# A T5-bias table for dilated attention: rows stored once and repeated from DRAM to DRAM

## The chip, the core and the metric

The kernel runs on one core of a Trainium2 chip, in one launch. The metric is the time of the whole program on the device in microseconds (us), lower is better. Five engines work side by side, each in its own order and tied to the others by semaphores: TensorE (PE, with its weight loads as PEld), VectorE (DVE), ScalarE (ACT), GpSimd (POOL) and SyncE (SP, which only issues transfers). Transfers are issued by SP, ACT or POOL into their own queues and carried out by DMA engines.

## The reference

One decoder layer over 2048 tokens of width 1024. What matters here is the input projection and the bias of the dilated attention:

```python
proj = h @ w_in[i]
r_in, k_in, v_in, q_at, k_at, v_at = jnp.split(proj, splits, axis=-1)
y_rwkv = rwkv7_mix(h, r_in, k_in, v_in, ...)
y_att = dilated_attention(to_heads(q_at), to_heads(k_at), to_heads(v_at), rel_bias)

def dilated_branch(q, k, v, rel_bias, window, dil):    # for (128, 1), (512, 4), (2048, 16)
    ...
    rel = np.arange(blk)[:, None] + blk - np.arange(2 * blk)[None, :]
    bias = jnp.transpose(rel_bias[t5_bucket(np.clip(rel, 0, None) * dil)], (2, 0, 1))
    logits = jnp.einsum('bdhnqc,bdhnkc->bdhnqk', qs, kb) * (HEAD_DIM ** -0.5) + bias[None, None, :, None]
    logits = jnp.where(valid, logits, NEG_INF)
```

For each of three patterns and each of 8 heads the bias depends on the distance of query and key alone, so one row of 384 numbers holds all of it; a block of 128 queries by 256 keys reads that row with a shift of one for each query. After the attention come an output projection, layer norms, a router with 32 experts, and a gated embedding.

## The kernel before, in words

The program goes through stages: `project` (the input projection, and the preparation of the RWKV inputs), `mixers` (RWKV and attention woven together), `mix_out`, `route`, `ple`, `experts`, `finish`. Products of float32 are made of three matmuls of split operands (lines 196 to 200).

The change is in the part of `project` that makes the RWKV keys and the attention values (lines 455 to 488), some 350 to 590 us from the start. It runs in steps. A step makes one 128x512 piece of the key (24 matmuls; ScalarE writes a scaled copy `sh` at L285, VectorE adds into `o` at L287, SP stores `o` at L290), squares it on ScalarE (`sq`, L458), makes two pieces of the values (24 matmuls each; ScalarE copies them to `ov`, L452; SP stores them, L453), and between these the norm of the key: PE sums `sq` into `pn` (L462), VectorE and ScalarE make the reciprocal root, and SP stores `rn` (L468). Four steps make one column block of the key weights. In each four, SP loads the weights of the next block (`wr`, L255).

The tiles `sh`, `ov` and others share one tag of the pool `st` with two buffers, so a tile waits until the one two places back is free, and an `ov` is free when its store has landed.

The bias table is made beside these steps by a generator, `attn_bias`. At the end of each step the loop calls it once (`next(bias, None)`, L486), and it runs to its next `yield`. For a pattern it loads constants on POOL's queue, multiplies them on PE (L965), subtracts on VectorE (L966) into `br` (8 partitions, a head each, of 384 numbers), and stores `br` 128 times over on ACT's queue (L967) into the DRAM tensor `biasrow` (8 heads, 3 patterns, 128 rows, 384). Much later `load_bias` (L995) reads from it with a row step of 383, which gives the shift, 128x2x256 for two heads.

PE's order in `project` is that of the code (`manual_schedule`); the other engines' order, and all in `mixers`, is set by a scheduler that simulates the program. Transfers from SP and ACT take eight completion semaphores in turn (named DMAHW0 to DMAHW7 below); before a transfer takes one again, its queue waits until the last transfer that used it has landed.

Of the kernel before, what the change touches and what calls it, by code (L numbers as in the profile page):

```python
# [18 lines left out]
P = 128  # L19
# [148 lines left out]
class K:  # L168
# [784 lines left out]
    def attn_bias(self, tile, bank):  # L953

        nc, I = self.nc, self.I
        L = 3 * P
        self.biasrow = rows = self.scratch("biasrow", (8, 3, P, L))
        for n in range(3):
            hot, br = tile(32, L + 8, "hot"), tile(8, L, "br")
            nc.gpsimd.dma_start(hot[:, 0:L], I["hot"][:, n])  # L960
            nc.gpsimd.dma_start(hot[:, L:], I["rel_bias"])
            nc.gpsimd.dma_start(br, I["gone"][:, n])
            yield
            ps = bank()
            nc.tensor.matmul(ps[0:8, 0:L], hot[:, L:], hot[:, 0:L], start=True, stop=True)  # L965
            nc.vector.tensor_tensor(out=br, in0=br, in1=ps[0:8, 0:L], op=ALU.subtract)  # L966
            nc.scalar.dma_start(rows[:, n], br.unsqueeze(1).to_broadcast([8, P, L]))  # L967
            yield
            yield
            yield  # L970

    def attn_open(self, es):
        self.al, self.ap = (es.enter_context(self.tc.tile_pool(name=name, bufs=1, reuse_waits="tile")) for name in ("al", "ap"))
# [1022 lines left out]
```

## Time and profile before

| | |
|---|---|
| time, median of 3 runs | 3246.5 us (3241.99 to 3250.48) |
| the profiled execution | 3253.92 us, its span 3252.1 us |
| PE busy | 2928.5 us, 90% of the span |
| VectorE, ScalarE busy | 2113.1 us, 1526.9 us |
| DMA, mean | 164 GB/s |
| mean granted TensorE clock | 0.928 of full speed |
| the three bias stores | 1536 KB each, issued at 373.1, 437.5 and 502.0 us |

Times inside the program count from the start of the span. A wait is the idle time of an engine ahead of an instruction, put down to what ended it. In a row of the timeline the bracket gives that wait. The queue of SP's transfers is q1, that of ACT's is q10.

### The profile page before, as it was taken

How to read it: one execution, taken by the hardware profiler on the slowest of the kernel's cores; microseconds unless marked ns; L12 is line 12 of the kernel's file. 1: busy time of each engine (PE TensorE's matmuls, PEld its weight loads, DVE VectorE, ACT ScalarE, POOL GpSimd, SP SyncE). 2: the span in 40 equal slices, each digit the busy share in tenths (PEclk: the TensorE clock that was granted, in tenths of full speed). 3: DMA queues.
4: the chain of work that ended last, by engine and by line, in shares of the span. 5: the costliest groups of instructions: out<-in, count | busy, mean ns of one | idle time of the engine just before them, and what ended most of it. 6: DMA issues, size and time to landing. Idle time of an engine off the chain costs nothing. (4 is left out here: it accounts for less than half of the span.)

```text
span 3252.1 us, 49914 instructions
## 1 busy us (share of the span) xinstructions
PE 2928.5 (90%) x17038; PEld 2335.2 (72%) x17039; DVE 2113.1 (65%) x4730; ACT 1526.9 (47%) x3650; POOL 675.3 (21%) x682
## 2 busy tenths in 40 slices
PE   8989888999798998998997899899999999998880
PEld 6666777777687777777786677788777777776560
DVE  4997333686564755666657678653587787766756
ACT  3444211555454544544444233311477777765642
POOL 0442000244100312112102122223011111112216
PEclk9999989999799889988898899999999999999885
DMA  5212433688725335235205453243499999987845
GB/s 166 80 56 95 103 88 80 203 273 266 154 60 123 100 79 132 69 76 139 65 22 144 138 177 123 96 140 94 175 307 323 324 304 322 313 295 225 289 130 210
DMA packets 364064, 533.09 MB, mean 164 GB/s; under 512 B 92376, under 2 KB 204640, under 8 KB 363792
## 3 DMA queue, kind: packets, MB, share of 16 engines
q1 hardware_dynamic: 330144, 459.09, 44.4%
q0 software_dynamic: 14496, 45.93, 6.0%
q10 hardware_dynamic: 19168, 24.86, 3.1%
q8 instruction: 136, 2.23, 0.3%
q14 instruction: 120, 0.98, 0.1%
HBM read 402.27 MB, written 128.06 MB: 163 GB/s over the span
## 5 line engine op out<-in xcount | busy, mean ns | idle before, releaser
L1711 DVE TENSOR_TENSOR wl<-raw,wh 128x512 fp32r<-128x512 f32 x768 | 478.0, 681 | 88.5 <-ACT wh L1710 87.9
L1710 ACT CAST wh<-raw 128x512 fp32r<-128x512 f32 x768 | 417.5, 620 | 12.2 <-DMA raw<-in_w_up_dram 10.5
L198 PE MATMUL ps<-xh,wh 128*128 128x512 f32 x640 | 263.1, 411 | 0.3 <-ACT xh L322 0.3
L199 PE MATMUL ps<-xl,wh 128*128 128x512 f32 x640 | 259.2, 405 | 0.9 <-DVE xl L323 0.8
L200 PE MATMUL ps<-xh,wl 128*128 128x512 f32 x640 | 257.9, 403 | 0.0
L1088 ACT ACTIVATE pe<-pe,ms 128x256 f32<-128x256 f32 (+1 forms) x384 | 174.9, 457 | 161.0 <-DVE ms L1085 153.3
L1840 POOL DMA_INDIRECT acc<-ysb,ix x48 | 96.5, 2010 | 623.0 <-ACT ysb L1839 402.6
L198 PE MATMUL pe<-wh,XX 128*128 128x512 f32 x480 | 199.3, 415 | 3.8 <-ACT wh L1710 3.8
L199 PE MATMUL pe<-wl,XX 128*128 128x512 f32 x480 | 191.8, 400 | 2.6 <-DVE wl L1711 2.6
L200 PE MATMUL pe<-wh,XX 128*128 128x512 f32 x480 | 190.7, 397 | 0.0
L198 PEld LDWEIGHTS ps<-xh,wh 128*128 128x128 f32 x640 | 125.1, 195 | 34.2 <-issue 2.8
L199 PEld LDWEIGHTS ps<-xl,wh 128*128 128x128 f32 x640 | 124.7, 195 | 29.9 <-DVE xl L323 2.3
L200 PEld LDWEIGHTS ps<-xh,wl 128*128 128x128 f32 x640 | 124.5, 194 | 29.6
L1094 PE MATMUL pl<-eye,pe 128*128 128x128 f32 x600 | 128.6, 307 | 10.1 <-ACT pe L1088 9.5
L1069 PE MATMUL pl<-KK,Q 128*128 128x256 f32 x432 | 116.4, 395 | 20.3 <-DMA KK<-ks 8.2
L1108 PE MATMUL po<-pe,V 128*64 128x128 f32 x1200 | 123.0, 309 | 8.6 <-DVE O L1122 7.0
L198 PE MATMUL pb<-gh,XH 128*128 128x512 f32 x320 | 126.0, 394 | 0.0
L199 PE MATMUL pb<-gl,XH 128*128 128x512 f32 x320 | 125.2, 391 | 0.0
L1755 PE MATMUL pe<-wh,XX 128*128 128x512 f32 x288 | 120.1, 417 | 5.4 <-ACT wh L1710 5.4
L200 PE MATMUL pb<-gh,XL 128*128 128x512 f32 x320 | 124.8, 390 | 0.0
L1756 PE MATMUL pe<-wl,XX 128*128 128x512 f32 x288 | 118.4, 411 | 3.0 <-DVE wl L1711 3.0
L198 PE MATMUL pa<-woh,YH 128*128 128x512 f32 x256 | 112.5, 439 | 3.1 <-ACT YH L1338 3.1
(418 smaller groups left out, 7565.2 us busy)
## 6 DMA issues: line engine op xcount, KB each, us to landing
raw<-in_w_gate_dram SPq DMA_DIRECT2D x128, 512.0 KB
raw<-in_w_up_dram SPq DMA_DIRECT2D x128, 512.0 KB
raw<-in_w_down_dram SPq DMA_DIRECT2D x128, 512.0 KB
pk<-pk SPq DMA_DIRECT2D x32, 512.0 KB
pk_t<-pk SPq DMA_DIRECT2D x32, 512.0 KB
KK<-ks SPq DMA_DIRECT2D x64, 256.0 KB
wr<-in_w_in_dram SPq DMA_DIRECT2D x48, 256.0 KB
rkk<-rkk SPq DMA_DIRECT2D x32, 384.0 KB
```

The costliest lines, as they stand in the source:

```text
L198: mm(out, lh, rh, start=first, stop=False)
L199: mm(out, lh, rl, start=False, stop=False)
L200: mm(out, ll, rh, start=False, stop=last)
L1069: mm(pl[:, h], q, toks(KK[:, m, h], n, prev, 2), start=m == 0, stop=m == 1)
L1088: nc.scalar.activation(pe[:, h, w], pe[:, h, w], AF.Exp, bias=m_[h], scale=-1.0, accum_out=s_[h])
L1094: nc.tensor.transpose(pt[:, h, b], pe[:, h, b * P:(b + 1) * P], self.c("eye"))
L1108: mm(o[h * 64:(h + 1) * 64, j], vb[:, h * 64:(h + 1) * 64], tt[:, h, b], start=b == kb[0], stop=b == 1)
L1710: nc.scalar.copy(wh[:, c], raw[:, c])
L1711: nc.vector.tensor_tensor(out=wl[:, c], in0=raw[:, c], in1=wh.bitcast(F32)[:, c], op=ALU.subtract)
L1755: mm(ps, L[:, 0:P], wh, start=first, stop=False)
L1756: mm(ps, L[:, 0:P], wl, start=False, stop=last)
L1840: nc.gpsimd.indirect_dma_start(out=self.acc, out_offset=bass.IndirectOffsetOnAxis(ap=ix[0:r, e, b:b + 1], axis=0), in_=ysb[0:r], in_offset ...
```

## The change

`attn_bias` stores `br` once, 8 rows of 384 numbers, into a new DRAM tensor `biasone`. In its next two turns it issues four copies from there to `biasrow`, DRAM to DRAM, two heads each and 128 times over, two in each turn. The number of turns for a pattern stays at four. All five transfers are on ACT's queue.

```diff
         self.biasrow = rows = self.scratch("biasrow", (8, 3, P, L))
+        one = self.scratch("biasone", (8, 3, L))
         for n in range(3):
...
             nc.vector.tensor_tensor(out=br, in0=br, in1=ps[0:8, 0:L], op=ALU.subtract)
-            nc.scalar.dma_start(rows[:, n], br.unsqueeze(1).to_broadcast([8, P, L]))
+            nc.scalar.dma_start(one[:, n], br)
             yield
-            yield
-            yield
+
+            for h in range(0, 8, 2):
+                nc.scalar.dma_start(rows[h:h + 2, n], one[h:h + 2, n].unsqueeze(1).to_broadcast([2, P, L]))
+                if h % 4:
+                    yield
```

ScalarE at the first pattern, before (semaphores that an instruction waits for stand in brackets; PE_49, DVE_49 and Activation_49 are the engines' own):

```order
L452 COPY ov<-ps 128x256 [waits PE_49,Activation_49]
L967 DMA biasrow<-br 8x128x384 [waits DMAHW2_49,DVE_49]
L285 ACTIVATE sh<-ps,prm 128x512 [waits DMAHW0_49,PE_49,Activation_49]
L458 ACTIVATE sq<-o,prm 128x512 [waits DVE_49]
L452 COPY ov<-ps 128x256 [waits DMAHW1_49,PE_49,Activation_49]
```

And the same place with the change (lines behind 967 are moved by up to 4):

```order
L452 COPY ov<-ps 128x256 [waits PE_49,Activation_49]
L968 DMA biasone<-br 8x384 [waits DMAHW2_49,DVE_49]
L972 DMA biasrow<-biasone 2x128x384 [waits DMAHW2_49]
L972 DMA biasrow<-biasone 2x128x384
L972 DMA biasrow<-biasone 2x128x384 [waits DMAHW6_49]
L285 ACTIVATE sh<-ps,prm 128x512 [waits DMAHW0_49,PE_49,Activation_49]
L972 DMA biasrow<-biasone 2x128x384 [waits DMAHW7_49]
L458 ACTIVATE sq<-o,prm 128x512 [waits DVE_49]
L452 COPY ov<-ps 128x256 [waits DMAHW1_49,PE_49,Activation_49]
```

The scheduler put three of the four copies right behind the small store and the fourth behind `sh`; the first copy waits for the small store (DMAHW2).

SP's queue behind that place, before, from the store of `rn` in the step of the bias store on:

```order
L468 DMA rkk<-rn 128x512 [waits DMAHW3_49,DVE_49]
L290 DMA rkk<-o 128x512 [waits DMAHW4_49,DVE_49]
L453 DMA va<-ov 128x256 [waits DMAHW5_49,Activation_49]
L453 DMA va<-ov 128x256 [waits DMAHW6_49,Activation_49]
L468 DMA rkk<-rn 128x512 [waits DMAHW7_49,DVE_49]
L255 DMA wr<-in_w_in_dram 128x4x128 [waits DMAHW0_49,DVE_49]
L255 DMA wr<-in_w_in_dram 128x4x128 [waits DMAHW1_49,DVE_49]
L290 DMA rkk<-o 128x512 [waits DMAHW2_49,DVE_49]
L453 DMA va<-ov 128x256 [waits DMAHW3_49,Activation_49]
```

And with the change:

```order
L468 DMA rkk<-rn 128x512 [waits DMAHW3_49,DVE_49]
L290 DMA rkk<-o 128x512 [waits DMAHW0_49,DVE_49]
L453 DMA va<-ov 128x256 [waits DMAHW1_49,Activation_49]
L453 DMA va<-ov 128x256 [waits DMAHW2_49,Activation_49]
L468 DMA rkk<-rn 128x512 [waits DMAHW3_49,DVE_49]
L255 DMA wr<-in_w_in_dram 128x4x128 [waits DMAHW4_49,DVE_49]
L255 DMA wr<-in_w_in_dram 128x4x128 [waits DMAHW5_49,DVE_49]
L290 DMA rkk<-o 128x512 [waits DMAHW6_49,DVE_49]
L453 DMA va<-ov 128x256 [waits DMAHW7_49,Activation_49]
```

The order on SP is the same. Its semaphores are others: the bias store had DMAHW2, and the copies now have DMAHW4 to DMAHW7, which the last four rows wait for.

In `mixers` rows change their neighbours. PE near its begin, before (`pl` are attention's products, the others RWKV's):

```order
L1069 MATMUL pl_7362<-KK,Q 128x256
L822 MATMUL ps_7369<-pk_t 128x128 x4
L834 MATMUL ps_7555<-eye,v_t 128x128 x2
L725 MATMUL ps_7559<-eye,pk_t 128x128 x2
L822 MATMUL ps_7370<-pk_t 128x128 x4
L1072 MATMUL pl_7344<-KK,Q 128x256 x2
L1069 MATMUL pl_7355<-KK,Q 128x256 x3
```

And with the change:

```order
L1073 MATMUL pl_7375<-KK,Q 128x256
L822 MATMUL ps_7382<-pk_t 128x128 x4
L834 MATMUL ps_7568<-eye,v_t 128x128 x2
L725 MATMUL ps_7572<-eye,pk_t 128x128 x2
L1076 MATMUL pl_7357<-KK,Q 128x256 x2
L1073 MATMUL pl_7368<-KK,Q 128x256 x3
L1073 MATMUL pl_7375<-KK,Q 128x256 x3
L822 MATMUL ps_7383<-pk_t 128x128 x4
```

Products of attention stand here ahead of four matmuls of RWKV that were ahead of them; there are more such exchanges down to the end of the stage, and no instruction is added or taken away there.

## Rows read from the trace of the kernel before

**Rows 1.** The page, busy time of each engine.

```profile
PE 2928.5 (90%) x17038; PEld 2335.2 (72%) x17039; DVE 2113.1 (65%) x4730; ACT 1526.9 (47%) x3650; POOL 675.3 (21%) x682
```

**Rows 2.** Stretches around the first bias store: length, busy time, clock, DMA share.

```profile
core 0: us, PE busy (x) PEld busy (x) DVE busy (x) ACT busy (x) POOL busy (x), PEclk, DMA share, GB/s
376.00:390.00 14.00, 14.00 (x88) 12.26 (x87) 4.86 (x4) 3.66 (x7) 0.00 (x0) 1.00 0.52 77
390.00:404.00 14.00, 2.18 (x19) 1.97 (x17) 2.68 (x5) 1.27 (x3) 0.00 (x0) 0.71 0.50 76
404.00:410.00 6.00, 5.53 (x22) 4.50 (x23) 2.72 (x2) 1.42 (x3) 0.52 (x1) 0.55 0.68 183
```

**Rows 3.** Waits from 370 to 425: total us, times, longest.

```profile
POOL br L962 <- DMA biasrow<-br: 35.8, 1, 35.8
DVE sh L284 <- DMA va<-ov: 15.3, 1, 15.3
PE pn L462 <- ACT sq L458: 12.3, 1, 12.3
ACT sh L285 <- DMA va<-ov: 10.7, 1, 10.7
```

**Rows 4.** Timeline of ScalarE from 362 to 447: start, us, what.

```profile
365.71 0.72 ACT L458 ACTIVATE sq<-o,prm 128x512 f32<-128x512 f32 x1 [0.82 <-DVE o L287]
...
373.10 0.55 ACTq L967 DMA_DIRECT2D biasrow<-br  x1
377.29 0.69 ACT L285 ACTIVATE sh<-ps,prm 128x512 f32<-128x512 f32 x1 [6.15 <-PE ps L200]
378.79 0.72 ACT L458 ACTIVATE sq<-o,prm 128x512 f32<-128x512 f32 x1 [0.82 <-DVE o L287]
...
400.97 0.69 ACT L285 ACTIVATE sh<-ps,prm 128x512 f32<-128x512 f32 x1 [10.70 <-DMA va<-ov]
...
443.15 0.73 ACT L458 ACTIVATE sq<-o,prm 128x512 f32<-128x512 f32 x1 [0.82 <-DVE o L287]
```

**Rows 5.** SP's issues: timeline, then all stores of L453.

```profile
367.45 4.04 SPq L453 DMA_DIRECT2D va<-ov  x2
373.76 0.32 SPq L468 DMA_DIRECT2D rkk<-rn  x1
378.79 0.32 SPq L290 DMA_DIRECT2D rkk<-o  x1
...
384.26 3.69 SPq L453 DMA_DIRECT2D va<-ov  x1
...
L453 SPq DMA_DIRECT2D va<-ov x32: 319/320/3837, 355.3 to 589.6; - x32
```

**Rows 6.** Timeline of ScalarE from 546 to 572, undisturbed steps.

```profile
547.08 0.73 ACT L458 ACTIVATE sq<-o,prm 128x512 f32<-128x512 f32 x1 [0.82 <-DVE o L287]
559.21 0.72 ACT L458 ACTIVATE sq<-o,prm 128x512 f32<-128x512 f32 x1 [0.82 <-DVE o L287]
571.33 0.73 ACT L458 ACTIVATE sq<-o,prm 128x512 f32<-128x512 f32 x1 [0.82 <-DVE o L287]
```

**Rows 7.** Waits from 360 to 560: PE, then SP's queue.

```profile
PE pn L462 <- ACT sq L458: 36.7, 3, 12.3
...
SPq L290 <- DMA biasrow<-br: 3.6, 3, 1.2
```

**Rows 8.** DMA queues from 373 to 411: packets, MB, share of 16 engines.

```profile
q10 hardware_dynamic: 1032, 1.57, 35.9%
```

**Rows 9.** The same of SP's queue, one store of 1 KB rows (371.6:372.6), one of 2 KB (361.9:363.1).

```profile
q1 hardware_dynamic: 144, 0.13, 37.4%
...
q1 hardware_dynamic: 144, 0.26, 57.5%
```

**Rows 10.** The same of ACT's queue from 22 to 23.4, mostly `slotlist`.

```profile
q10 hardware_dynamic: 68, 0.70, 119.1%
```

**Rows 11.** POOL: its issue ahead of `br`, and DMA issues from 360 to 560.

```profile
372.23 0.50 POOL L961 DMA_DIRECT2D hot<-in_rel_bias_dram  x1
...
hot<-in_rel_bias_dram POOLq DMA_DIRECT2D x2, 1.0 KB, 1.8
br<-in_gone_dram POOLq DMA_DIRECT2D x2, 12.0 KB, 3.0
```

**Rows 12.** Issues with `biasrow`: ns min/median/max, first and last start.

```profile
L1002 SPq DMA_DIRECT2D bias<-biasrow x12: 360/371/537, 814.7 to 1553.7; - x12
L967 ACTq DMA_DIRECT2D biasrow<-br x3: 271/290/548, 373.1 to 501.9; - x3
```

**Rows 13.** The stretch of attention and RWKV, columns as in rows 2.

```profile
815.00:1720.00 905.00, 843.67 (x7196) 682.17 (x7193) 548.45 (x2053) 433.45 (x1500) 136.51 (x250) 0.90 0.38 91
```

**Rows 14.** ACT's issues of `mul`: ns min/median/max, first and last start.

```profile
L242 ACTq DMA_DIRECT2D mul<-in_mu_lora_dram x3: 447/1252/2491, 8.6 to 11.3; - x3
```

## The prediction

> **What bounds the kernel now.** I read the page's totals first: TensorE (PE) is busy 90% of the span, so an edit to the bias rows is worth something only where PE stands still because of them [rows 1]. Then the stretches around the first of the three bias stores, issued at 373.10 (called T from here). The reader is to see PE full until 390, 2.18 of 14 us busy from 390 to 404, and a granted clock of 0.55 just behind it, that is, mostly its lower level of 1.2 GHz instead of 2.4 [rows 2]. The waits of that stretch say what ended the stall: PE's `pn` waited 12.3 us for ScalarE's `sq`, VectorE and ScalarE waited 15.3 and 10.7 us for a store `va<-ov`, and POOL's next load of `br` waited 35.8 us for the bias store itself [rows 3]. So `sh` of L285, which needs the buffer of an `ov` two tiles back, starts at 400.97 = T+27.9 [rows 4]. The stores are ordinary ones of 128 KB. The one issued at 384.26 kept SP 3.69 us at its issue, against a median of 320 ns [rows 5].
>
> What such a stall costs comes from equal steps. Undisturbed, `sq` follows `sq` after 12.12 us (547.08 to 559.21 to 571.33) [rows 6]; with the small bias matmul in it a step takes 13.08 (365.71 to 378.79). Four steps with one such matmul are 3 x 12.12 + 13.08 = 49.4 us; from 378.79 to 443.15, with a bias store in them, they are 64.4 [rows 4, 6]. That is 15.0 us for each pattern, 45 us for three (PE's wait on `sq` is 36.7 us in three from 360 to 560, the longest 12.3 [rows 7]).
>
> **The change part by part.** What is removed: three stores of 1024 rows of 1536 B, read out of 8 partitions. The transfer queue of ACT (q10) shows 1032 packets from 373 to 411: 1024 rows and 8 short endings, while an SP store of 128 rows shows 144, that is 128 and 16 [rows 8, 9]. So a transfer whose first dimension is 8 ran on 8 of the 16 DMA engines, 128 rows on each, and the share of busy DMA engines of about a half agrees [rows 2]. One row took 35.9% x 16 x 38 us / 1032 = 212 ns.
>
> What is added: three stores of 12 KB, and twelve copies of 2 x 128 rows. The twelve are DRAM to DRAM, and their first dimension is 2.
>
> How many engines a copy gets is the main question. The row says 8 engines for 8 and 16 for 128, so I take two engines for 2, and 128 rows on each: all four copies of a pattern put 512 rows on the same two engines, where before 128 rows lay on each of eight.
> The Trainium skill, "DMA: Bandwidth & Descriptors", section "Rules for kernel authors", says that an outermost dimension of size c below 16 confines the whole transfer to at most c engines, and the section "Why a DMA increments its semaphore by 16 and not by 1" adds that they are the lowest-numbered ones. By that rule two engines carry all of it; the 1032 packets agree for c = 8, and no run here shows c = 2.
>
> What one row costs from DRAM to DRAM the trace doesn't show at this size. Nearest rows: SP's stores take 37.4% x 16 x 1 us / 128 = 47 ns for 1 KB and 57.5% x 16 x 1.2 us / 128 = 86 ns for 2 KB [rows 9], so 1.5 KB lies near 65 ns. The only DRAM to DRAM copy of the kernel, `slotlist`, fills most of a stretch with 119.1% x 16 x 1.4 us for 0.70 MB (packets count where they begin), 38 us/MB, or 59 ns for a row [rows 10]. The upper end is the 212 ns of now. I take 65, since both nearest rows lie there and the 212 belongs to eight engines reading eight neighbouring partitions; 59 and 212 stay as ends.
>
> The sum for one pattern, from T: the small store issues in 0.3 us and lands in about 2.5 (POOL's transfers of 1 KB and 12 KB land in 1.8 and 3.0 [rows 11]); three issues take some 0.6 us until the first rows run; then 512 x 65 ns = 33.3 us. The last row is through at T+36.7. ScalarE waits for the landing of the small store, T+0.3 to T+2.8; its next work is `sh` at T+4.2 [rows 4], so that wait is covered, with 1.4 us left.
>
> Now the SP stores behind these rows. Each is spread over all 16 engines, so it ends only when its share on the two engines is through. Before, the store was released at T+27.9, 7.5 us ahead of the end of POOL's wait for the bias store (372.7 + 35.8 = T+35.4) [rows 3, 4, 11], that is with some 35 of 128 rows left. With 35 rows of 65 ns left, 2.3 us ahead of T+36.7, the release is T+34.4; an undisturbed `sh` would be at T+16.3 (377.29 + 12.1). So the stall stays and ends 6.5 us later than now; I take 6, since part of the copies may be issued later and let a store in between. Three patterns: +18 us. The tail with the low clock stays as it is. Twelve issues against three, at 0.27 to 0.55 us each as now [rows 12], lie in the same stall.
>
> Where a copy goes on the queue matters too. SP's transfers take eight completion semaphores in turn, and a transfer waits for the last one that used its own; SP already waits for `biasrow<-br` in this way, 3.6 us in three times [rows 7]. Now two loads `wr`, a store `rkk<-o` and the next step's first `va<-ov` stand in turn behind the four copies. Behind that `va<-ov` on SP everything is queued, and the `sh` of the second step waits for it. If the first stall has already cost 18 us, that store is due at T+38 and loses nothing much.
>
> Moved: the bias loads of attention come 400 us later (814.7 at the earliest [rows 12]) and don't notice. In attention and RWKV (815 to 1720 us) the scheduler gives many rows another neighbour; the instructions are the same, and PE is busy 843.67 of 905 us there [rows 13]. I take 0 and bound it by a sixth of the 61 us that are idle: 10 us either way.
>
> Sum: the profiled execution took 3253.9 us (span 3252.1), so it would be 3272. That execution is 7.4 us above the median of the runs, 3246.5; on the median the forecast is 3246.5 + 18 = **3265 us**.
>
> **The rivals.**
> (a) The stores of SP slip in between the rows, and only the semaphores hold. A store may be 9.8 us late before `sh` feels it (`ov` stored at 367.45, its buffer taken by `sh` at 377.29 [rows 4, 5]). For: in the stretch of the bias store SP's rows did get through in part, since two of its stores were issued in the normal 0.32 us [rows 5]. Against: the 15.3 us wait. Then the last copy lands at T+36.7 plus 2.5 for SP's own share and 2 to land, T+41; the `va<-ov` behind it lands at T+44; the `sh` that needs it would be at T+28.4; 15.6 us late, against 11.6 now (400.97 against 389.4): +4 for a pattern, +12, 3258 us. At 59 ns a row, 3.1 us less: +3, 3249.
> The Trainium skill, "DMA: Bandwidth & Descriptors", section "Queues, rings and completion order", says that a DMA engine goes round its queues packet by packet, 9 to 17 rows typical, 64 at most. By that a store would wait 1.1 to 4.2 us at 65 ns, and this rival would hold; today's 15.3 us wait stands above the 64 x 212 ns = 13.6 us that the same rule gives, so the trace speaks for it only at its ceiling.
> (b) Faster: the copies are spread over all 16 engines and the stall goes. For: what makes a row cost 212 ns now may be the eight source partitions, and they are gone. A pattern's 1024 rows would be 64 rows on each engine, 4.2 us, under the slack of 9.8. It gives back 45 us: 3202. Against: the eight endings. It decides from four times as many endings; on two engines a row would have to cost under 51 ns for any gain ((27.9 - 3.4) / 477), below every row measured.
> (c) A row from DRAM to DRAM costs what it costs now, 212 ns: 108 us for a pattern, which is longer than the 64 us between patterns. By the sum of (a) the `va<-ov` lands near T+119, 91 us late and 79 more than now for a pattern: +237, 3484 us. For it: each row is read and written in DRAM. Against: `slotlist`.
> (d) ScalarE is held at the issue. Of three element-wise loads in a row the third issue took 2491 ns [rows 14]; a third and fourth copy may wait 4 to 8 us each until an earlier one's rows are handed out, and `sh` and `sq` stand behind them. PE then stops earlier, but the end of the pattern is still set by the 512 rows, so it is inside the forecast's range.
>
> **How the numbers follow.** Forecast with (d) 0.52 (+10 to +30), (a) 0.22 (+2 to +12), (b) 0.14, (c) and other prices over 85 ns 0.12. Leaving out (b) and the dear end of (c) leaves about 0.78 inside. Low end: (a) at 59 ns, +3, less the 10 of the moved rows, 3239. High end: 85 ns a row (the price of 2 KB), 10 us more for a pattern than at 65: 3246.5 + 18 + 30 = 3295. I call 0.3%, some 10 us, what a measurement can tell. Faster is (b) and a sliver of (a), 0.16; within 0.3% is most of (a) and the low edge of the forecast, 0.20; slower the rest, 0.64.
>
> **What would show it.** In the profile after: q10 with 128 + 128 rows and 2 endings for each copy, 1032 packets and some 16 more for a pattern, with a DMA share near 0.2 instead of 0.5 for over 30 us behind each small store. PE's wait on `sq` stays at 12 us or more, or splits in two, three times; the wait named is `va<-ov` or `biasrow<-biasone`, on SP too. 16 endings a copy, or a PE without a gap at 385 to 410, would make the forecast wrong; a share of 0.2 for 100 us would be (c).

## The result, and the profile after

The changed kernel takes 3267.9 us (median of 10 runs) against 3246.4 of the kernel before: ratio 1.0054, 95% interval 1.0035 to 1.0072, so some 11 to 23 us slower. One of the ten runs of the kernel before took 8884 us; it hardly moves the median and has no part in the ratio. Run again (experiment 8) the ratio was 1.0070 [1.0044, 1.0096]. The forecast was 3265 and slower. The time was right, and so was the length of the transfers; the step by which they were to cost it was not.

The stretches around the first pattern, to be read beside [rows 2] (the small store is now issued at T = 371.94, 1.2 us earlier than the bias store before; columns as there):

```profile
376.00:390.00 14.00, 2.90 (x25) 2.69 (x23) 0.81 (x2) 0.69 (x1) 0.00 (x0) 0.69 0.18 66
390.00:404.00 14.00, 10.52 (x46) 8.65 (x47) 4.81 (x4) 1.99 (x4) 0.00 (x0) 0.70 0.23 84
404.00:410.00 6.00, 5.63 (x37) 4.73 (x36) 2.31 (x4) 2.71 (x5) 0.00 (x0) 1.00 0.49 158
```

TensorE used to stop from 390 to 404; now it stops from 376 to 390, in the very step of the small store. The DMA share is 0.18 to 0.23 instead of 0.5: few engines are at work, for longer. The granted clock is 0.69 and 0.70 in the first two stretches, so partly at its lower level of 1.2 GHz, and back at 2.4 GHz in the third.

Who waits, from 370 to 425, against [rows 3] (total us, times, longest):

```profile
PE pn L462 <- ACT sq L458: 15.0, 2, 14.6
ACT sh L285 <- issue: 14.4, 1, 14.4
...
ACT sq L458 <- issue: 7.7, 1, 7.7
```

No wait for `va<-ov` is left. ScalarE's `sh` and `sq` are late, and "issue" says that ScalarE waited for nothing that the profile shows. Its own timeline shows what it did (start, us, what; against [rows 4]):

```profile
364.55 0.72 ACT L458 ACTIVATE sq<-o,prm 128x512 f32<-128x512 f32 x1 [0.82 <-DVE o L287]
...
371.94 0.54 ACTq L968 DMA_DIRECT2D biasone<-br  x1
373.35 10.86 ACTq L972 DMA_DIRECT2D biasrow<-biasone  x3
384.33 0.69 ACT L285 ACTIVATE sh<-ps,prm 128x512 f32<-128x512 f32 x1 [14.35 <-issue]
384.36 8.30 ACTq L972 DMA_DIRECT2D biasrow<-biasone  x1
392.70 0.72 ACT L458 ACTIVATE sq<-o,prm 128x512 f32<-128x512 f32 x1 [7.68 <-issue]
...
406.12 0.68 ACT L285 ACTIVATE sh<-ps,prm 128x512 f32<-128x512 f32 x1
...
431.75 0.72 ACT L458 ACTIVATE sq<-o,prm 128x512 f32<-128x512 f32 x1 [0.82 <-DVE o L287]
```

Three issues take 10.86 us and the fourth 8.30, where an issue took 0.27 to 0.55 [rows 12]. ScalarE stands in them, and `sh`, `sq`, the matmuls of `pn` behind `sq`, and all later products stand behind ScalarE. From `sq` at 364.55 to `sq` at 431.75 four steps take 67.2 us, against 64.4 before and 49.4 undisturbed.

SP's stores by line, against the last row of [rows 5], where one issue took 3837 ns:

```profile
L453 SPq DMA_DIRECT2D va<-ov x32: 319/320/339, 354.2 to 596.2; - x32
```

SP's waits on the copies' semaphores from 360 to 560, against the second of [rows 7]:

```profile
SPq L453 <- DMA biasrow<-biasone: 3.5, 3, 1.7
```

And ScalarE's transfer queue from 373 to 411, against [rows 8] (packets, MB, share of 16 engines):

```profile
q10 hardware_dynamic: 1032, 1.57, 11.2%
```

No store of L453 is held at its issue now, and SP waits 1.7 us at most for a copy. The 1032 packets are 1024 rows and two endings for each of the four copies (the small store's 16 lie ahead of 373). So each copy runs on 2 engines, and a row takes 11.2% x 16 x 38 / 1032 = 66 ns.

How far the loss lies in this stage is read from two rows: the sixteen `sq` of L458, and the first load of a bias block (first and last start). After:

```profile
L458 ACT ACTIVATE sq<-o,prm x16: 721/723/726, 352.4 to 591.0; 128x512 f32<-128x512 f32 x16
...
L1006 SPq DMA_DIRECT2D bias<-biasrow x12: 359/370/537, 829.4 to 1573.7; - x12
```

And before:

```profile
L458 ACT ACTIVATE sq<-o,prm x16: 721/724/726, 353.5 to 584.3; 128x512 f32<-128x512 f32 x16
```

The stage from the first `sq` to the sixteenth takes 238.6 us against 230.8: +7.8, or +2.6 for a pattern. From there to the first bias load it is 238.4 against 230.4 (814.7 [rows 12]): another +8. From that load to the end of the span it is 2435.8 against 2437.4.

### The profile page after: what moved, and what is told of

Same layout as the page of the kernel before. It is cut to its first block, busy times and chain, and to the rows that moved or that the text cites. A ratio compares the mean times of both kernels' runs of the same rounds, so it can differ in the third digit from the quotient of the medians.

```text
span 3265.2 us, 49921 instructions
## 1 busy us (share of the span) xinstructions
PE 2932.6 (90%) x17038; PEld 2338.0 (72%) x17039; DVE 2111.6 (65%) x4730; ACT 1530.2 (47%) x3650; POOL 675.3 (21%) x682
```

## The experiments

Called A here is the theory that ScalarE is held at the issue; B is the prediction's step, that SP's stores stand behind the rows; C is that SP waits for semaphores which copies hold; D is that a row is dear. T is the issue of the small store, "the stage" the time from the first to the sixteenth `sq`. Where the stop is gone (experiments 1, 2, 4, 7 and 10) the stage came out at 187.5 to 188.2 us, so the bias stores of before cost 43 us in it and the copies of the changed kernel 51.

**1. The same twelve copies, rows first.** Every other instruction stands as in the changed kernel; the first dimension of a copy is 128 instead of 2.

```diff
-                nc.scalar.dma_start(rows[h:h + 2, n], one[h:h + 2, n].unsqueeze(1).to_broadcast([2, P, L]))
+                nc.scalar.dma_start(rows[h:h + 2, n].rearrange("h i l -> i h l"), one[h:h + 2, n].unsqueeze(0).to_broadcast([P, 2, L]))
```

> The same twelve copies, issued at the same places in the same order on every engine, but with the 128 rows as the first dimension (128x2x384 instead of 2x128x384), so that 16 engines should share each. Theory A (ScalarE is held at the issue of the third and fourth copy until the rows of earlier copies are handed out, and the 512 rows lie on two engines): a copy is 16 rows of 65 ns on each engine, 1 us; no issue over 1.2 us, PE's wait on sq gone, a pattern 49 to 50 us instead of 67, time 3195 to 3210. Theory B (the prediction's step: SP's stores end late behind the rows): the same, since 64 rows take 4.2 us of a slack of 9.8. Theory C (the waits on the semaphores that the copies took over): the same. Rival D (a row is dear because it is copied inside DRAM, whatever the number of engines): the issues stay long, 3240 or more.

Measured: 3221.9 us, ratio 0.9905 [0.9876, 0.9934], stage 187.6. The sixteen `sq`, and ScalarE's timeline:

```profile
L458 ACT ACTIVATE sq<-o,prm x16: 722/724/726, 349.4 to 537.0; 128x512 f32<-128x512 f32 x16
...
369.00 0.54 ACTq L968 DMA_DIRECT2D biasone<-br  x1
370.41 1.95 ACTq L972 DMA_DIRECT2D biasrow<-biasone  x3
373.18 0.69 ACT L285 ACTIVATE sh<-ps,prm 128x512 f32<-128x512 f32 x1 [6.15 <-PE ps L200]
373.20 0.54 ACTq L972 DMA_DIRECT2D biasrow<-biasone  x1
```

And its copies in the list of issues from 360 to 560 (KB each, median us from issue to landing):

```profile
biasrow<-biasone ACTq DMA_DIRECT2D x12, 384.0 KB, 5.7
```

Four issues take 2.5 us in all, `sh` is on time, and no stop is left. So neither the number of copies nor the moved order makes the stage long; two engines for 512 rows do. The time lies 12 us above the range that was expected: the kernel before took 3253.0 beside it, not 3246.4, and 236.8 us pass behind the stage, not 230.4 (see experiment 12). The same holds for experiments 2 and 4, 6 and 1 us above theirs.

**2. One copy of eight heads from DRAM.** The shape is that of the bias store before (8x128x384, eight endings, 128 rows on each engine); only the source has gone from 8 partitions of the on-chip memory to DRAM.

```diff
-            for h in range(0, 8, 2):
-                nc.scalar.dma_start(rows[h:h + 2, n], one[h:h + 2, n].unsqueeze(1).to_broadcast([2, P, L]))
-                if h % 4:
-                    yield
+            nc.scalar.dma_start(rows[:, n], one[:, n].unsqueeze(1).to_broadcast([8, P, L]))
+            yield
+            yield
```

> One copy of all eight heads for a pattern, heads first (8x128x384), from DRAM: the transfer of the kernel before with only its source changed, and with its order of instructions. If the 212 ns for a row of before came from reading eight neighbouring partitions: 65 ns a row, 128 rows on 8 engines in 8.3 us, under the slack of 9.8 us, stall gone, 3200 to 3210. If it came from eight engines writing at once or from the queue behind: 212 ns again and the stall of 12 us stays, 3240 to 3250. Theories A, B and C don't differ here (one issue, one semaphore, 8.3 us).

Measured: 3216.0 us, ratio 0.9887 [0.9858, 0.9916], stage 187.5. Queues from 373 to 390 (packets, MB, share of 16 engines):

```profile
q10 hardware_dynamic: 1048, 1.59, 27.0%
```

A packet takes 27.0% x 16 x 17 / 1048 = 70 ns against 212 [rows 8], and by 386.0, 11.9 us after the issue at 374.13, all 1048 have begun, where the bias store of before took some 35 us to land. What made the stores of before dear was their source, not the number of their engines.

**3. The 512 rows on 2 engines, but in one issue.** A 16-engine copy makes the table; a second one writes 2x512 rows to a tensor that nobody reads.

```diff
+        more = self.scratch("biasmore", (3, 2, 4 * P + 1, L))
...
-            for h in range(0, 8, 2):
-                nc.scalar.dma_start(rows[h:h + 2, n], one[h:h + 2, n].unsqueeze(1).to_broadcast([2, P, L]))
-                if h % 4:
-                    yield
+            nc.scalar.dma_start(rows[:, n].rearrange("h i l -> i h l"), one[:, n].unsqueeze(0).to_broadcast([P, 8, L]))
+            nc.scalar.dma_start(more[n, :, 0:4 * P], one[0:8:4, n].unsqueeze(1).to_broadcast([2, 4 * P, L]))
+            yield
+            yield
```

> The table is made by one copy over 16 engines; behind it ScalarE issues one copy of 2x512 rows into a tensor that nobody reads: the 512 rows on two engines of the changed kernel, in one issue instead of four. Theory A: ScalarE is held nowhere (two issues, each under 1.5 us), PE doesn't wait on sq by more than 2 us, 3200 to 3212. Theory B: SP's stores behind the 512 rows come late as predicted, sh starts near T+34 (T: the small store's issue) with DVE and ACT waiting on va<-ov, 3255 to 3268. Theory C: the first step goes on, and the va<-ov of the next step stands on SP until the big copy lands at T+39, sh of the second step 13 us late, 3250 to 3262.

Measured: 3280.6 us, ratio 1.0085 [1.0057, 1.0112], stage 246.9. ScalarE's timeline:

```profile
370.74 0.62 ACTq L972 DMA_DIRECT2D biasrow<-biasone  x1
371.40 0.66 ACTq L973 DMA_DIRECT2D biasmore<-biasone  x1
373.52 0.69 ACT L285 ACTIVATE sh<-ps,prm 128x512 f32<-128x512 f32 x1 [6.15 <-PE ps L200]
...
386.41 0.68 ACT L285 ACTIVATE sh<-ps,prm 128x512 f32<-128x512 f32 x1
...
416.61 0.69 ACT L285 ACTIVATE sh<-ps,prm 128x512 f32<-128x512 f32 x1 [23.09 <-DMA va<-ov]
```

And SP's waits from 360 to 560:

```profile
SPq L453 <- DMA biasmore<-biasone: 78.0, 3, 26.4
```

With ScalarE free, the `sh` that B makes late (that of the next step) is on time at 386.41, while the same 512 rows run on the same 2 engines. B falls. The step after it is late by C: SP's store waits up to 26.4 us for the semaphore of the big copy, and three such waits cost 59 us of stage, more than the hold that they replace. So C has the wait, but not its size: the time lies 19 us above the range expected of it. In the changed kernel that wait is 1.7 us at most, because ScalarE's hold has delayed everything ahead of it. So 512 rows on 2 engines cost 50 to 60 us here by either way, and taking one stop out brings in the other.

**4. The changed kernel's copies, issued by POOL.**

```diff
-                nc.scalar.dma_start(rows[h:h + 2, n], one[h:h + 2, n].unsqueeze(1).to_broadcast([2, P, L]))
+                nc.gpsimd.dma_start(rows[h:h + 2, n], one[h:h + 2, n].unsqueeze(1).to_broadcast([2, P, L]))
```

> The twelve copies of 2x128x384 are issued by POOL instead of ScalarE, in the order of instructions of the kernel before; SP's semaphores are those of the kernel before too. Theory A: ScalarE is free, no stall, 3200 to 3215, as long as POOL's own next loads aren't late. Theory B: if they run on two engines, 33 us for a pattern, SP's stores behind them come late, stall of 12 to 18 us, 3245 to 3268. Theory C: no semaphore of SP is held by a copy, no stall, 3200 to 3215.

Measured: 3216.0 us, ratio 0.9883 [0.9853, 0.9912], stage 187.7. POOL's timeline:

```profile
375.31 4.32 POOL L972 DMA_DIRECT2D biasrow<-biasone  x4 [2.03 <-DMA biasone<-br]
```

And the copies in the list of issues from 360 to 560:

```profile
biasrow<-biasone POOLq DMA_DIRECT2D x12, 384.0 KB, 13.5
```

Four issues take 4.32 us, and a copy lands in 13.5, where the fourth would need more than 33 if all lay on the same two engines. So this takes away both the hold on ScalarE and the pile on two engines, and does not tell the two apart.
The Trainium skill, "DMA: Bandwidth & Descriptors", section "Why a DMA increments its semaphore by 16 and not by 1", says that a transfer issued by GpSimd gets its few engines from a cursor that moves on, while one of SP's or ACT's always gets the lowest-numbered ones. The 13.5 us fit that; no run here shows which engines they were.

**5. One copy a step.** The copies were put into four successive steps, the last two of a pattern into the first two of the next (`copy(n, h)` is the changed kernel's copy of the heads `h` and `h + 1`).

```diff
             nc.gpsimd.dma_start(br, I["gone"][:, n])
+            if n:
+                copy(n - 1, 4)
             yield
+            if n:
+                copy(n - 1, 6)
...
+            copy(n, 0)
+            yield
+            copy(n, 2)
+            yield
...
```

> The changed kernel's twelve two-head copies, unchanged in shape (2x128x384), source, issuer (ScalarE) and engines (2), but one a step over four steps, the last two of a pattern in the next pattern's first two steps; nothing else is changed. Theory A (ScalarE is held at the issue of a copy while the two before it are not handed out): a copy takes 8.3 us and a step 12.1, so no issue finds two before it; each of the twelve issues under 2 us, no stall of TensorE over 2 us in the stage, the stage from the first sq to the sixteenth near 188 us against 238.6 in the changed kernel, and about 3216 to 3222 us as with the first, second and fourth experiment. Theory B (SP's stores stand behind rows on the 2 engines): the rows are as many and on the same 2 engines, so each of twelve steps has a store up to 8 us late; the stage stays long, 3245 to 3270. Theory C (waits on semaphores that the copies hold): the copies end 8 to 10 us after their issue, inside a step, so a few us at most, 3216 to 3230.

Measured: 3274.9 us, ratio 1.0074 [1.0047, 1.0101], stage 239.3. ScalarE's timeline:

```profile
371.29 11.12 ACTq L961 DMA_DIRECT2D biasrow<-biasone  x3
...
382.56 8.27 ACTq L961 DMA_DIRECT2D biasrow<-biasone  x1
```

The expectation failed because the edit did nothing: the scheduler sets ScalarE's order, the copies are ready as soon as the small store is in, and they stand on ScalarE exactly as before. It is in effect another measurement of the changed kernel and says nothing on the theories. The same holds for the two turns in which the change itself issues its copies: a `yield` in the source didn't hold a transfer back here.

**6. Two small copies behind the 512 rows.** What lets an issue go? The third experiment with two copies of 2 rows behind the big one.

```diff
...
             nc.scalar.dma_start(more[n, :, 0:4 * P], one[0:8:4, n].unsqueeze(1).to_broadcast([2, 4 * P, L]))
+            for k in (0, 2):
+                nc.scalar.dma_start(more[n, :, 4 * P + k:4 * P + k + 1], one[0:8:4, n].unsqueeze(1).to_broadcast([2, 1, L]))
```

> The third experiment with two copies of 2 rows behind the 512-row copy on ScalarE's queue (2x1x384, to rows of the tensor that nobody reads): four issues per pattern as in the changed kernel, in the order table (16 engines), 2x512 rows (2 engines), 2 rows, 2 rows. Tells what holds an issue. A by count (an issue is held while two copies before it are not handed out): the third is held until the table copy is through, about 8 us, and the fourth until the 512 rows are, about 45 us after the small store's issue, though each has 2 rows. A by the rows of the copy itself (a copy of many rows has to find room for them): the two small ones take under 1 us each, as the first two do. A by the rows that wait in all (some 256 to an engine): the third is held until half the 512 rows are out, about 28 us, and the fourth follows at once. The time is that of the third experiment, 3275 to 3290 by each, since the second step waits for the 512 rows there in any case.

Measured (one run): 3327.8 us, stage 279.5. ScalarE's timeline:

```profile
372.60 0.62 ACTq L972 DMA_DIRECT2D biasrow<-biasone  x1
...
373.96 30.54 ACTq L975 DMA_DIRECT2D biasmore<-biasone  x1
404.63 0.69 ACT L285 ACTIVATE sh<-ps,prm 128x512 f32<-128x512 f32 x1 [35.41 <-issue]
404.65 0.54 ACTq L975 DMA_DIRECT2D biasmore<-biasone  x1
```

And its queue from 373 to 404.5, the moment at which the third issue is let go:

```profile
q10 hardware_dynamic: 1838, 2.80, 27.1%
```

A copy of 2 rows is held for 30.54 us and the next one for none. That rules out a hold by the copy's own rows (under 1 us was expected of it), a hold by the number of copies (8 us, and 45 for the next) and a fixed price of an issue. What is left is the rows that wait in front: some 28 us and none for the next were expected of it. Of the 1838 packets 1024 are the table's rows and 16 its endings; 798 are rows of the big copy, 399 on each engine, so 113 of its 512 were still waiting. In the changed kernel the same count (its queue from 373 to 376.43, to 384.21 and to 392.66, the ends of the second, third and fourth issue) is:

```profile
q10 hardware_dynamic: 41, 0.06, 6.1%
...
q10 hardware_dynamic: 290, 0.44, 11.0%
...
q10 hardware_dynamic: 543, 0.83, 11.5%
```

Without the endings (none, 2, 4) that is 20, 144 and 270 rows on each engine, which leaves 108, 112 and 114 of the copy just ahead (128, 256 and 384 less these). So ScalarE's issue is let go when some 110 rows of the copy in front are left on an engine, four times over; the expectation had 256. The time is some 40 us above what was expected: the stage is 91.9 us longer than the undisturbed one, 30.6 for a pattern, which is the hold itself in the first step, where the third experiment's wait in the second step cost 59 us in all.

**7. One copy of all eight heads, rows first, 16 engines**, as a candidate for the best version.

```diff
-            for h in range(0, 8, 2):
-                nc.scalar.dma_start(rows[h:h + 2, n], one[h:h + 2, n].unsqueeze(1).to_broadcast([2, P, L]))
-                if h % 4:
-                    yield
+            nc.scalar.dma_start(rows[:, n].rearrange("h i l -> i h l"), one[:, n].unsqueeze(0).to_broadcast([P, 8, L]))
+            yield
+            yield
```

> One copy for all eight heads with the rows first (128x8x384, 16 engines, ScalarE issues it once per pattern), in the order of before; nothing is left out. Candidate for the best version. Theory A: one issue, not held; rows 1024 x 65 ns over 16 engines, 4 to 10 us beside the step's own transfers, so no stall in the stage: stage near 188 us, 3212 to 3222 us. Theory C: if the copy's end still comes after the step's next use of its semaphore, one or two us per pattern, up to 3225.

Measured: 3218.6 us, ratio 0.9883 [0.9858, 0.9908], stage 187.7: the same as the second, fourth and tenth experiment within their intervals. Sixteen engines are no better here than eight, since with eight the stop is gone already.

**8 and 9. The changed kernel and the kernel before once more**, for second profiles.

> The changed kernel once more, unchanged, for a second profile: does what it loses outside the twelve steps (2674.2 us from the sixteenth sq to the end of the span, against 2667.8 before) belong to it, or to the execution? If to the new order of the instructions: again 2674 or more with a stage of 238 to 239, and 3265 to 3270 us. If it is scatter between executions: anything from 2667 to 2680 as in the first four experiments, with the same stage.

> The kernel before, unchanged, for a second profile. In the first one the stretch from the sixteenth sq to the first load of a bias block takes 230.4 us; in the changed kernel 238.4 and 238.3, in the first to seventh experiment 234 to 239. If those 4 to 8 us belong to the copies from DRAM: again 229 to 232 here. If the first profile of before was a lucky execution: 234 to 239 here. The stage of the sixteen sq should again take 230 to 232 with three stalls of 12.3 us on TensorE.

Measured: the changed kernel 3278.4 us against 3258.0, stage 238.6, behind it 238.2 us to the first bias load; the kernel before 3242.9 (one run), stage 231.5, behind it 232.1. Rows of the kernel before, second profile:

```profile
L458 ACT ACTIVATE sq<-o,prm x16: 721/723/726, 351.7 to 583.2; 128x512 f32<-128x512 f32 x16
...
L1002 SPq DMA_DIRECT2D bias<-biasrow x12: 359/371/538, 815.3 to 1555.8; - x12
```

So the 6 to 8 us behind the stage repeat in a second pair of profiles. The stretch does vary: in experiments 1 to 7, 10 and 11, whose edits all lie ahead of it, it takes 234.2 to 242.3 us. From the first bias load on, before takes 2437.4 and 2425.8 us and after 2435.8 and 2436.1: there two profiles of one kernel differ by more than the two kernels do.

**10. Two copies of four heads.** Four engines, two issues.

```diff
-            for h in range(0, 8, 2):
-                nc.scalar.dma_start(rows[h:h + 2, n], one[h:h + 2, n].unsqueeze(1).to_broadcast([2, P, L]))
-                if h % 4:
-                    yield
+            for h in range(0, 8, 4):
+                nc.scalar.dma_start(rows[h:h + 4, n], one[h:h + 4, n].unsqueeze(1).to_broadcast([4, P, L]))
+                yield
```

> Two copies of four heads (4x128x384) per pattern in place of four of two heads, on ScalarE; 4 engines and 256 rows on each, against 2 engines and 512. Nothing is left out. Theory A, sized by the changed kernel's four held issues (each let go when 103 to 112 rows of the copy before were left on an engine): the second issue is let go after some 23 rows at 65 ns, 1.5 to 2.5 us; there is no third; ScalarE is free 4.5 us after the small store's issue and sh isn't late; no stall over 2 us in the stage, the stage 188 to 192 us, 3214 to 3225 us. Theory C (semaphores): the copies end some 19 us after the small store's issue, after the second step's use of ScalarE's queue, 2 to 4 us per pattern at most: up to 3232.

Measured: 3221.1 us, ratio 0.9876 [0.9847, 0.9906], stage 188.2. ScalarE's timeline:

```profile
374.50 3.24 ACTq L972 DMA_DIRECT2D biasrow<-biasone  x2
377.86 0.69 ACT L285 ACTIVATE sh<-ps,prm 128x512 f32<-128x512 f32 x1 [6.73 <-PE ps L200]
```

The two issues take 3.24 us together, as the first two of the changed kernel take 3.08, and `sh` is 0.6 us late (6.73 against 6.15). The hold is there, small, and the stage doesn't feel it. Its queue from 374.5 to 377.74, the end of the second issue, and SP's waits from 360 to 560:

```profile
q10 hardware_dynamic: 71, 0.11, 11.8%
...
SPq L453 <- DMA biasrow<-biasone: 11.4, 3, 4.0
```

That is 18 of 128 rows on each of four engines, so 110 are left: the same count a fifth time. And SP waits up to 4.0 us for a copy here without any loss of stage, so the 1.7 us of the changed kernel hardly explain its stop.

**11. Every copy doubled.** The added copies go to a tensor that nobody reads.

```diff
+        more = self.scratch("biasmore", (8, 3, P, L))
...
                 nc.scalar.dma_start(rows[h:h + 2, n], one[h:h + 2, n].unsqueeze(1).to_broadcast([2, P, L]))
+                nc.scalar.dma_start(more[h:h + 2, n], one[h:h + 2, n].unsqueeze(1).to_broadcast([2, P, L]))
```

> The changed kernel with every two-head copy followed by one like it to a tensor that nobody reads: eight issues per pattern, 1024 rows on each of 2 engines. Order on ScalarE: three issues, sh, three issues, sq, two issues. Theory A by rows (an issue is let go when some 105 rows of the copy before are left on an engine): the third at T+12 as now, the sixth at T+1.6+(5x128-105)x0.065 = T+37, the eighth at T+53, T being the small store's issue; sq waits some 24 us behind the sixth and TensorE stops for some 30 to 45 us per pattern instead of 15; the stage 320 to 345 us, 3345 to 3375 us. If the hold were a fixed price of an issue (5 to 8 us each, whatever is in front): the eighth at T+40 at the least, the stage 300 to 310.

Measured (one run): 3349.8 us, stage 313.7. ScalarE's timeline:

```profile
369.47 0.54 ACTq L969 DMA_DIRECT2D biasone<-br  x1
...
373.59 7.68 ACTq L973 DMA_DIRECT2D biasrow<-biasone  x1
...
381.42 8.27 ACTq L974 DMA_DIRECT2D biasmore<-biasone  x1
...
397.51 7.30 ACTq L974 DMA_DIRECT2D biasmore<-biasone  x1
404.86 0.72 ACT L458 ACTIVATE sq<-o,prm 128x512 f32<-128x512 f32 x1 [22.77 <-DMA biasmore<-biasone]
404.88 8.62 ACTq L973 DMA_DIRECT2D biasrow<-biasone  x1
413.63 8.00 ACTq L974 DMA_DIRECT2D biasmore<-biasone  x1
```

From the third on each issue costs 7.3 to 8.6 us, the time of 128 rows at 65 ns, and the eighth ends at T+52.2 (53 expected of A by rows). The stage was expected at 320 to 345 and came out at 313.7, 6 short of the low end. The T+40 expected of a fixed price of an issue took 5 us for each; at 8 us for each of six issues it would end the eighth near T+52 too. So this run doesn't tell rows from a fixed price; the sixth experiment does.

**12. The kernel before with the small store added**, for the 6 to 8 us behind the stage.

```diff
+        one = self.scratch("biasone", (8, 3, L))
...
+            nc.scalar.dma_start(one[:, n], br)
             nc.scalar.dma_start(rows[:, n], br.unsqueeze(1).to_broadcast([8, P, L]))
```

> The kernel before with the small store (8x384 to biasone, which nobody reads here) put ahead of each of its three big ones; the order of every engine is otherwise that of before. For what is lost behind the twelve steps: from the sixteenth sq to the first load of a bias block the two profiles of before take 230.4 and 232.1 us, those of the changed kernel 238.4 and 238.3, and the experiments with copies from DRAM 234 to 242, also where their order on every engine is that of before. If the added small store or the added tensor is enough for it (another turn of the queues' semaphores, another place in DRAM): 234 to 242 here too. If it hangs on the copies from DRAM themselves: 230 to 232. The stage itself should be that of before, 231 to 235 us with three stops of 12 us, some 1 to 3 us more per pattern if the big store's rows wait for the small one's, since the rows still come from 8 partitions at some 212 ns.

Measured (one run): 3265.8 us, against 3256.0 for before in one run beside it.

```profile
L458 ACT ACTIVATE sq<-o,prm x16: 722/725/727, 351.5 to 582.3; 128x512 f32<-128x512 f32 x16
...
L1004 SPq DMA_DIRECT2D bias<-biasrow x12: 360/370/537, 820.2 to 1572.2; - x12
```

The stage stays at 230.8 us; behind it 237.9 pass to the first bias load, as in the kernels with copies. So this loss doesn't seem to need the copies: with three stores of 12 KB and a tensor that nobody reads it is there, in one profile against two of before. Part of it may be the clock: TensorE is busy 224.9 us of the stretch here, at a granted clock of 0.94, against 223.4 at 0.94 and 221.4 at 0.96 in the two of before. Whether the turn of the completion semaphores does the rest, or the tensors' new places in DRAM, was not told apart.

## Why the prediction was right and where it was wrong

**Right: the transfers.** Two engines for a first dimension of 2, 65 ns a row (66 measured), 512 rows in 33 us, four copies through at T+36.7 (1029 of the 1032 packets have begun by 408.8, T+36.9). So the 212 ns belonged to the source, as taken (experiment 2), and that TensorE would not get its time back hung on the two engines: the same copies on 16 engines lose nothing in the stage (experiment 1). Rivals (b) and (c) are out.

**Wrong: what waits for them.** The step that SP's stores stand behind these rows, so that `sh` is released at T+34.4, failed. No `sh` waits for a store behind these rows, in the changed kernel or in the third experiment; where a store came late there, it had waited for a semaphore. What held the stage was rival (d): ScalarE is held at the third copy until the first and some 16 rows of the second are out, at the fourth until the second and some 14 of the third are, and `sh` and `sq` stand behind the issues. The step was read off the stores of before, which were late behind rows of 212 ns (15.3 us); experiment 2 shows that this lateness went with the dear rows, and by what turn the engines served the two queues is left open. The prediction had the hold of ScalarE, with 4 to 8 us an issue (8 measured), but counted it as inside the forecast's range because "the end of the pattern is still set by the 512 rows". It isn't: the second step's `sh` runs at T+34.2 (406.12) by a sum of its own, ScalarE free at T+20.8 and one more step behind, and that it falls beside T+34.4 is a coincidence. Experiment 10 shows why it mattered: by (d) the price falls to nothing with half the rows on an engine.

**Wrong in size: +6 for a pattern.** It is +2.6 in the stage (7.8 in three). A pattern costs 17.8 us (67.2 - 49.4): TensorE's waits on `sq` are 15.0 of it, the longest 14.6, and the other 2.8 fall near them, where the granted clock is 0.69 and 0.70; what they are made of was not told apart.

**Missing: 6 to 8 us behind the stage.** The prediction put 0 there and bounded only the mixers, where nothing is to be seen. Experiment 12 points to the added store or tensor, by one profile. The forecast of +18 is thus 8 of the stage and about 7 behind it, and came near the measured 17.5 (0.54% of 3246.4) by two errors that cancel, which is luck. Rival (a), that SP's semaphores hold, is real at 1.7 us; with ScalarE out of the way it becomes the bound (experiment 3).
The Trainium skill, "DMA: Bandwidth & Descriptors", section "Queues, rings and completion order", says that a DMA engine goes round its queues packet by packet. SP's punctual stores in the third experiment agree with it, and so with rival (a) more than with the forecast.

**The change's idea was good, its cut was not.** Repeating the rows from DRAM takes the stop away entirely if the rows are spread over four engines or more, or issued by POOL: 3216 to 3222 us in experiments 1, 2, 4, 7 and 10, ratios 0.9876 to 0.9905. The two-head cut gave all of that back. Among those five the intervals overlap; one copy of eight heads (experiment 2) is the simplest.

## What to carry to other kernels

When a transfer is cut into pieces, work out for each the engines that its first dimension allows and add up the rows on the fullest engine: in these runs the sum, not the number of pieces or where they stand in the source, set how long the semaphores were taken, and it held the issuing engine at every further issue behind the piled-up rows (a single issue of 512 rows held nobody at its own issue, experiment 3). If rows come out of few partitions many times over, store them once and repeat them from DRAM. A wait "issue" on an engine that also computes is read from its own timeline, where the long issue stands.

## What the runs showed of the hardware that was not expected

- A row of 1536 B out of 8 partitions took 212 ns, from DRAM 70, also on eight engines.
- An issue by ScalarE was let go when some 110 rows of the transfer in front were left on an engine (108, 110, 112, 113, 114), even one of 2 rows that had nothing else against it (30.54 us).
- With a store of 12 KB added three times, the 230 us behind the stage came out 6 to 8 us longer (one profile against two); by what was not shown.
